# Banded attention with both key triangles in one square, in a two-layer decoder on one core

## The chip, the core and the metric

The kernel runs on one NeuronCore of a Trainium2 chip. The core has five engines that run side by side, each through its own queue in order: TensorE (PE, matmuls into PSUM, with its weight loads listed as PEld), VectorE (DVE), ScalarE (ACT), GpSimd (POOL) and SyncE (SP, which issues DMAs here). An instruction starts when it is at the head of its engine's queue and the semaphores it waits for have come. The metric is the device time of one launch in microseconds (us).

## What is computed

A trunk of two layers over 512 tokens of 1024 features, in float32. Layer 0 mixes positions with a gated MLP, layer 1 with windowed attention; both have a gated feed-forward part and a per-layer embedding. The change is in the attention of layer 1:

```python
def mixer_b(xn, w_q, sinks, w_o, kblk, vblk):
    q = (xn @ w_q).reshape(B, nb, BLOCK, N_KV_HEADS, GQA_GROUP, HEAD_DIM)
    scores = jnp.einsum('bnikgd,bnjkd->bnkgij', q, kblk) * (HEAD_DIM ** -0.5)
    dist = i + BLOCK - j
    in_band = (dist >= 0) & (dist < WINDOW)
    valid = in_band[None] & ((blk > 0) | (j[None] >= BLOCK))
    scores = scores - slopes * dist
    scores = jnp.where(valid, scores, -jnp.inf)
    m = jnp.maximum(jnp.max(scores, axis=-1, keepdims=True), sink)
    e = jnp.exp(scores - m)
    probs = e / (jnp.sum(e, axis=-1, keepdims=True) + jnp.exp(sink - m))
    out = jnp.einsum('bnkgij,bnjkd->bnikgd', probs, vblk)
    return out.reshape(B, S, N_Q_HEADS * HEAD_DIM) @ w_o
```

There are 16 query heads of 64 features in 4 groups, which share 4 key/value heads; 4 blocks of 128 queries; and a window of 128 keys. A query i of a block sees the keys j <= i of its own block and the keys j > i of the block before: two triangles that together fill one 128 x 128 square. The first block has no block before it. Each head has a sink, a logit without a value.

## The kernel before

Activations lie with features on the 128 partitions and tokens along the free axis. Every matrix product is made of three matmuls: a float32 number is split into a high half (rounded to the format in which PE multiplies at full pace) and a low half, and the products high x high, high x low and low x high are summed in PSUM. So each weight piece that a DMA brings (`wraw`) is cast by ScalarE (`wh`, line 157) and subtracted by VectorE (`wl`, line 158). `plan` lists the pieces in order of use, `load` issues their DMAs on SP's queue into three buffers of 8 KB per partition, and `pump` does the two splits up to four units of 1024 columns ahead of PE.

PSUM has eight banks of 512 columns, and all tiles rotate through them (`psum`). The order on each queue follows the program, moved a little by a scheduler: it puts instructions that are ready by its own estimate ahead, and `tc.high_priority()` lets a block go first.

The attention is a loop of 16 steps (line 786), one for a group g and a block n, with stages that overlap: at step i the scores of step i, the transposes of step i-1 and the value product of step i-2. Between them stands other PE work from a table, `beside`: the query projections of the later groups (`project`), the values of the later blocks (`values`) and the first parts of the output projection (`merge`).

- `scores` (line 701): per head, two matmuls of up to 256 columns against the keys of the previous and the own block (`kh`, `kl`), a fused VectorE operation that adds the position table `far` (with a huge distance outside the band), scales, and gives the minimum; then the exponential on ScalarE with its sum. `nsink` is the sink with its sign turned.
- `weights` (line 730): the sink's share, the reciprocal, and the multiplication, two heads on ScalarE and two on VectorE.
- `turn` (line 743): four transposes by PE for each of the two key blocks, then the split into halves (`ph`, `pl`, `pts`).
- `mix` (line 760): six matmuls of 256 columns for each key block, against value tiles `vth` and `vtl`, in which zeros stand beside the values so that two heads land on different partitions; then the split into `o2`.

The queries of group 0 are written by ScalarE and VectorE into place; those of later groups go through DMAs from SBUF to SBUF (`queries`). After the loop the output projection is finished, added to the residual `h`, and the next norm begins (`nf`, with sums of squares `nf1acc` on GpSimd). Further places with names used below: the value projections of layer 0 (`v`, into eight PSUM tiles, with the norm's `n0ms` between), and, at the end, the transposes of the residual (`ht`) between the gate's matmuls.

Of the kernel before, what the change touches and what calls it, by code (L numbers as in the profile page):

```python
# [9 lines left out]
F32R = mybir.dt.float32r  # L10
AF = mybir.ActivationFunctionType
# [32 lines left out]
UNIT = 1024  # L44
WBUFS = 4
# [5 lines left out]
def tile_yoco(ctx: ExitStack, tc: tile.TileContext, t, out: bass.AP, out_b: bass.AP):  # L51
# [15 lines left out]
    pieces = []  # L67

    def plan(ap_, n, cols, own=None):

        if own and len(own) > 1:
            m = n // len(own)
            cuts = [(q * m, m) for q in range(len(own))]
        else:
            m = n if n <= UNIT else (n // cols + 1) // 2 * cols
            cuts = [(0, m), (m, n - m)] if m < n else [(0, n)]
        pieces.append((ap_, n, cuts, own))
# [10 lines left out]
    def plan_ffn(l):  # L88
        for i, (j0, j1) in enumerate(PARTS):
            if i == 0:  # L90
                plan_cols(t["w_up"][l], j1, KD)
            else:
                plan_cols(t["w_up"][l, j0 + 1 : j1], j1 - j0 - 1, KD)
            if i + 1 < len(PARTS):
                plan_cols(t["w_up"][l, j1 : j1 + 1], 1, KD)
            else:
                plan(t["pT"][l], 2 * S, S, own=[(mp, "m4", "m5")])
                plan_cols(t["w_pin"][l], 2, 4)
            plan_cols(t["w_down"][l], 4, j1 - j0, k0=j0)
# [14 lines left out]
    plan_cols(t["w_o"], 4, KD)  # L114
# [7 lines left out]
    units = [(i, q, lo, n) for i, p in enumerate(pieces) for q, (lo, n) in enumerate(p[2])]  # L122
    raws, ready = {}, {}
    state = {"raw": 0, "unit": 0, "next": 0, "tags": [0, 1, 2], "turn": 0, "pt": 0}

    def load(upto, queue=nc.sync):
        while state["raw"] < min(upto, len(pieces)):
            j = state["raw"]
            a, m = pieces[j][:2]
            tags = state["tags"]  # L130
            r = wp.tile([P, 2 * UNIT], F32, tag=f"r{tags[state['turn'] % len(tags)]}", bufs=1, name=f"wraw{j}")
# [9 lines left out]
    def pump(upto):  # L141
        while state["unit"] < min(upto, len(units)):
            i, q, lo, n = units[state["unit"]]
            load(i + 1)
            u = state["unit"]
            own = pieces[i][3]
            if own:
                pool, *tags = own[q]
# [4 lines left out]
            src = raws[i][:, lo : lo + n]  # L153
# [57 lines left out]
    for i, (k0, k1) in enumerate(FIRST[1:]):  # L211
        load(i + 2)
        for k in range(k0, k1):
            nc.sync.dma_start(h[k], t["xT"][k])
    nc.sync.dma_start(vec[:, KD:], t["vec"][:, KD:])
# [266 lines left out]
    far = const.tile([P, 2 * P], F32, name="far")  # L482
    nc.gpsimd.iota(far, pattern=[[1, 2 * P]], base=-P, channel_multiplier=-1,
                   allow_small_or_imprecise_dtypes=True)
    nc.gpsimd.affine_select(out=far, in_=far, pattern=[[-1, 2 * P]], compare_op=ALU.is_ge,
                            fill=-FAR, base=P, channel_multiplier=1)
    nc.gpsimd.affine_select(out=far, in_=far, pattern=[[1, 2 * P]], compare_op=ALU.is_ge,
                            fill=-FAR, base=-1, channel_multiplier=-1)

    qscale = const.tile([P, KD], F32, name="qscale")  # L490
    for hd in range(HEADS):
        nc.gpsimd.memset(qscale[hd % 2 * HD : (hd % 2 + 1) * HD, hd // 2 : hd // 2 + 1], 1.0 / (8.0 * slope(hd)))
# [8 lines left out]
    nc.gpsimd.tensor_scalar_mul(nsink, sink, -1.0)  # L501

# [68 lines left out]

# [12 lines left out]
    rt = nm.tokens()  # L584

# [5 lines left out]
    mm3(qps[1], parts, xq, P)  # L591

    for j in range(2):
# [9 lines left out]
    def queries(ps, g, j):  # L603


        qf = tp.tile([P, S], F32, tag="sq", name=f"qf{g}_{j}")
        m = 2 * g + j
        nc.vector.scalar_tensor_tensor(qf, ps, qscale[:, m : m + 1], rstd, op0=ALU.mult, op1=ALU.mult)
        res = [tp.tile([P, S], F32R, tag=("hs", "sg", "c0", "c1")[2 * j + e], name=f"q{g}_{j}_{e}")
               for e in range(2)]  # L610
        if g == 0:
            for e, q in enumerate(res):
                me, it = sides[e], sides[1 - e]
                nc.scalar.copy(q[me, :], qf[me, :])
                nc.vector.tensor_sub(q[it, :], qf[me, :], q[me, :].bitcast(F32))
            return res

        hi = tp.tile([P, S], F32, tag="acc", name=f"qhi{g}_{j}")
        nc.scalar.copy(hi.bitcast(F32R), qf)
        nc.vector.tensor_sub(qf.bitcast(F32R), qf, hi)  # L620
        for e, q in enumerate(res):
            me, it = sides[e], sides[1 - e]
            nc.sync.dma_start(q[me, :].bitcast(F32), hi[me, :])
            nc.sync.dma_start(q[it, :].bitcast(F32), qf[me, :])
        return res

    qs = {0: []}
    for j in range(2):
        qs[0] += queries(qps[j], 0, j)

    VW = (NC * GROUPS * 2 + 1) * HD
    vt = [wp.tile([P, VW], F32R, tag="r2", bufs=1, name="vth"), at.tile([P, VW], F32R, tag="vtl", name="vtl")]
    for x, eng in zip(vt, (nc.gpsimd, nc.vector)):
        eng.memset(x[:, : VW - HD].rearrange("p (b w) -> p b w", w=2 * HD)[:, :, :HD].bitcast(F32), 0.0)
        eng.memset(x[:, VW - HD :].bitcast(F32), 0.0)

# [3 lines left out]
    def values(c):  # L642
        if c == 0:
            box["v"] = chunk(256, KD)
        ps = psum(f"vv{c}")
        mm3t(ps[:, :256], xkv, box["v"], 0, 256, c)
        pg = ps[:, :256].rearrange("p (g d) -> p g d", g=GROUPS)
        vh, vl = (x[:, : VW - HD].rearrange("p (c g w) -> p c g w", c=NC, g=GROUPS)[:, c, :, HD:] for x in vt)
        nc.scalar.activation(vh, pg, AF.Copy, scale=rt[:, c : c + 1])
        nc.vector.scalar_tensor_tensor(vl, pg, rt[:, c : c + 1], vh.bitcast(F32),  # L650
                                       op0=ALU.mult, op1=ALU.subtract)

    def project(g, j, k0, k1):
        if j == 0 and k0 == 0:
            box["q"] = chunk(256, KD)
            qs[g] = []
        if k0 == 0:
            box["qp"] = psum(f"q{g}_{j}")
        mm3(box["qp"], box["q"][k0:k1], xq[k0:k1], j * P, first=k0 == 0, last=k1 == KD)
        if k1 == KD:  # L660
            qs[g] += queries(box["qp"], g, j)

    def merge(m, k0, k1):

        if m // 2 not in box:
            box[m // 2] = chunk(256, KD)
        if k0 == 0:
            box[f"o{m}"] = psum(f"o{m}")
        mm3(box[f"o{m}"], box[m // 2][k0:k1], o2[k0:k1], m % 2 * P, first=k0 == 0, last=k1 == KD)
        box[f"k{m}"] = k1  # L670

    beside = {
        -1: [(values, 0), (values, 1)],
# [332 lines left out]
```

## Time and profile before

| | |
|---|---|
| median of 3 runs | 1159.05 us (1155.9 to 1159.5) |
| profiled execution, whole | 1159.21 us |
| its span in the profile | 1157.5 us |
| mean granted clock of TensorE | 0.993 |
| instructions | 13692 |
| weight traffic | HBM read 108.24 MB, 95 GB/s over the span |

A profile row for a group of instructions reads: line, engine, operation, what is written <- what is read, shapes, count | busy us, mean ns of one | idle time of the engine just before them and what ended it. A row of a timeline begins with the start and the length in us. A matmul's length reaches from its start until its results are in PSUM, and matmuls overlap, so their pace is read from starts, or from the chain of waits, where only the time that a link adds is counted.

### The profile page before, as it was taken

How to read it: one execution, taken by the hardware profiler on the slowest of the kernel's cores; microseconds unless marked ns; L12 is line 12 of the kernel's file. 1: busy time of each engine (PE TensorE's matmuls, PEld its weight loads, DVE VectorE, ACT ScalarE, POOL GpSimd, SP SyncE). 2: the span in 40 equal slices, each digit the busy share in tenths (PEclk: the TensorE clock that was granted, in tenths of full speed). 3: DMA queues.
4: the chain of work that ended last, by engine and by line, in shares of the span. 5: the costliest groups of instructions: out<-in, count | busy, mean ns of one | idle time of the engine just before them, and what ended most of it. 6: DMA issues, size and time to landing. Idle time of an engine off the chain costs nothing.

```text
span 1157.5 us, 13692 instructions
## 1 busy us (share of the span) xinstructions
PE 1139.6 (98%) x5408; PEld 956.2 (83%) x5408; DVE 744.3 (64%) x1138; ACT 524.3 (45%) x850; POOL 85.1 (7%) x92
## 2 busy tenths in 40 slices
PE   9999999999999999999999999999999999999996
PEld 7888888888888888888889888888888888888895
DVE  7356477763676377457868876677626763675666
ACT  6534344432443244555567874444413432445542
POOL 2100210000000000022300002100000000000232
PEclk9999999999999999999999999999999999999998
DMA  9322322322322333232133314232232233234302
GB/s 320 123 75 73 109 93 89 110 102 81 109 89 80 110 103 115 88 108 91 41 87 110 97 32 173 83 109 97 86 109 95 78 101 109 91 99 138 110 1 73
DMA packets 30735, 115.41 MB, mean 100 GB/s; under 512 B 3016, under 2 KB 14928, under 8 KB 21200
## 3 DMA queue, kind: packets, MB, share of 16 engines
q1 hardware_dynamic: 29552, 113.37, 29.3%
q10 hardware_dynamic: 1120, 1.18, 0.3%
q8 instruction: 42, 0.69, 0.3%
q14 instruction: 21, 0.17, 0.0%
HBM read 108.24 MB, written 2.11 MB: 95 GB/s over the span
## 4 chain that ended last, share of the span: by engine, by line
PE 93%; DVE 2%; DMA 1%; POOL 1%; issue 1%; ACT 1%; SPq 0%; POOLq 0%; ACTq 0%
PE up L186 14%; PE up L185 14%; PE up L184 14%; PE d L186 8%; PE d L185 8%; PE d L184 8%; PE gate L184 2%; PE gate L186 2%; PE gate L185 2%; PE pv L773 1%; PE o L184 1%; PE o L185 1%; PE o L186 1%; PE u L185 1%; PE u L184 1%; PE u L186 1%
## 5 line engine op out<-in xcount | busy, mean ns | idle before, releaser
L158 DVE TENSOR_TENSOR wl<-wraw,wh 128x1024 fp32r<-128x1024 f32 (+2 forms) x197 | 237.8, 1209 | 130.7 <-ACT wh L157 120.7
L157 ACT CAST wh<-wraw 128x1024 fp32r<-128x1024 f32 (+1 forms) x196 | 201.5, 1032 | 235.6 <-PE d L185 131.6
L184 PE MATMUL up<-nf00h,wh 128*128 128x512 f32 x352 | 137.1, 390 | 0.0
L184 PE MATMUL up<-nf10h,wh 128*128 128x512 f32 x352 | 137.0, 389 | 0.0
L185 PE MATMUL up<-nf00l,wh 128*128 128x512 f32 x352 | 136.9, 389 | 0.0
L185 PE MATMUL up<-nf10l,wh 128*128 128x512 f32 x352 | 136.9, 389 | 0.0
L186 PE MATMUL up<-nf00h,wl 128*128 128x512 f32 x352 | 136.9, 389 | 0.0
L184 PE MATMUL d<-ah,wh 128*128 128x512 f32 x352 | 136.9, 389 | 0.0
L185 PE MATMUL d<-al,wh 128*128 128x512 f32 x352 | 136.9, 389 | 0.0
L186 PE MATMUL d<-ah,wl 128*128 128x512 f32 x352 | 136.9, 389 | 0.0
L186 PE MATMUL up<-nf10h,wl 128*128 128x512 f32 x352 | 136.9, 389 | 0.0
L361 ACT ACTIVATE c<-hs,vec 128x512 f32<-128x512 f32 x88 | 71.6, 814 | 85.8 <-DVE hs L357 85.0
L362 DVE SCALAR_TENSOR_TENSOR c<-hs,vec,c 128x511 f32<-128x511 f32 x88 | 65.8, 748 | 35.8 <-ACT c L361 35.6
L335 DVE TENSOR_TENSOR h<-h,d 128x512 f32<-128x512 f32 x56 | 38.4, 686 | 74.1 <-PE d L186 74.1
L245 ACT CAST ah<-a 128x512 fp32r<-128x512 f32 x44 | 27.3, 621 | 114.8 <-DVE a L367 114.8
L184 PEld LDWEIGHTS up<-nf10h,wh 128*128 128x128 f32 x352 | 66.1, 188 | 13.8
L184 PEld LDWEIGHTS d<-ah,wh 128*128 128x128 f32 x352 | 66.1, 188 | 13.8
L185 PEld LDWEIGHTS up<-nf00l,wh 128*128 128x128 f32 x352 | 66.1, 188 | 13.7
L185 PEld LDWEIGHTS d<-al,wh 128*128 128x128 f32 x352 | 66.1, 188 | 13.7
L185 PEld LDWEIGHTS up<-nf10l,wh 128*128 128x128 f32 x352 | 66.1, 188 | 13.7
L186 PEld LDWEIGHTS up<-nf00h,wl 128*128 128x128 f32 x352 | 66.1, 188 | 13.7
L184 PEld LDWEIGHTS up<-nf00h,wh 128*128 128x128 f32 x352 | 66.1, 188 | 13.6
(309 smaller groups left out, 2078.7 us busy)
## 6 DMA issues: line engine op xcount, KB each, us to landing
wraw<-in_w_up SPq DMA_DIRECT2D x44, 1024.0 KB, 4.8
wraw<-in_w_down SPq DMA_DIRECT2D x16, 896.0 KB, 4.6
wraw<-in_w_down SPq DMA_DIRECT2D x8, 1024.0 KB, 5.1
wraw<-in_w_u SPq DMA_DIRECT2D x4, 1024.0 KB, 6.5
wraw<-in_w_out SPq DMA_DIRECT2D x4, 1024.0 KB, 4.9
wraw<-in_w_gate SPq DMA_DIRECT2D x4, 1024.0 KB, 4.8
wraw<-in_w_q SPq DMA_DIRECT2D x4, 1024.0 KB, 5.0
wraw<-in_w_o SPq DMA_DIRECT2D x4, 1024.0 KB, 6.2
```

Source lines behind the costliest of these rows:

```text
L157: nc.scalar.copy(wh[:, :n], src)
L158: nc.vector.tensor_sub(wl[:, :n], src, wh[:, :n].bitcast(F32))
L184: nc.tensor.matmul(ps, wh[:, a:b], xh, start=st, stop=False)
L185: nc.tensor.matmul(ps, wh[:, a:b], xl, start=False, stop=False)
L186: nc.tensor.matmul(ps, wl[:, a:b], xh, start=False, stop=en)
L245: nc.scalar.copy(hi, src)
L335: nc.vector.tensor_add(h[m], h[m], ps)
L361: nc.scalar.activation(c, hs, AF.Identity, bias=v("conv_b", l * 2 * NJ + col), scale=cw[2])
L362: nc.vector.scalar_tensor_tensor(c[:, 1:], hs[:, : S - 1], cw[1], c[:, 1:], op0=ALU.mult, op1=ALU.add)
L773: nc.tensor.matmul(ps, lhs, rhs[:, :, e, :], start=first, stop=end)
```

## The change

It rewrites the attention loop, its preparation, the PSUM pool and the loads.

- **One square.** The scores of four heads go to one PSUM tile of two banks (`psum2`). Where j > i, `copy_predicated` copies the previous block's scores over the own block's (mask `above`), so that one square of 128 keys holds both triangles. One `scalar_tensor_tensor` for four heads multiplies by `rq` (the query's norm and 1/8) and adds `alibi` (slope times distance, made by GpSimd once per group); one `tensor_reduce` takes the minimum. The sink is a 129th column, so its exponential and sum come with the others. In the first block of a group the triangle j > i is filled with a huge number (`away`).
- **Weights and transposes.** The multiplication by the reciprocal is one GpSimd operation for four heads. There are four transposes per step, not eight; ScalarE makes the high half, VectorE the low one, and GpSimd's `affine_select` makes copies of both with only the triangle j > i.
- **Values.** A value tile holds the high and low halves side by side in 128 columns (`vt`), so one weight load serves both; `vd` holds the previous block's values minus the own block's, in the same way. A step is `vt` x all weights + `vd` x the triangle: four matmuls of 512 columns (two in a first block). The rows from the low halves then lie on partitions 64 to 127: ScalarE copies them down (`low_rows`) and VectorE adds (`outputs`).
- **Order.** All values are computed ahead of the loop; the queries of all groups go through DMAs; `beside` now has single products of the projection (three matmuls) and half output projections (`w_o` is planned in two halves, and each half is added to `h` by itself). High priority is gone.
- **PSUM.** Two banks belong to the scores; the other six rotate as four `mm`, one `tr`, one `pv`.
- **Loads.** Each unit of up to 1024 columns has its own DMA and buffer: six buffers of 4 KB per partition for three of 8 KB.

```diff
-    mmp = ctx.enter_context(tc.tile_pool(name="mmp", bufs=8, space=bass.MemoryType.PSUM))
-    def psum(name):
-        return mmp.tile([P, S], F32, tag="mm", name=name)
+    banks = {"at": 0, "tags": ["mm", "mm", "mm", "mm", "tr", "pv"]}
+    def psum(name, tag=None):
+        if tag is None:
+            tag = banks["tags"][banks["at"] % len(banks["tags"])]
+            banks["at"] += 1
+        return mmp.tile([P, S], F32, tag=tag, bufs=4 if tag == "mm" else 1, name=name)
+    def psum2(name):
+        return mmp.tile([P, 2, S], F32, tag="sc", name=name)
...
-    plan_cols(t["w_o"], 4, KD)
+    for k0 in (0, 4):
+        plan_cols(t["w_o"], 4, 4, k0=k0)
...
-            r = wp.tile([P, 2 * UNIT], F32, tag=f"r{tags[state['turn'] % len(tags)]}", bufs=1, name=f"wraw{j}")
+            r = wp.tile([P, UNIT], F32, tag=f"r{tags[state['turn'] % len(tags)]}", bufs=1, name=f"wraw{j}")
...
+    def halves(dst, src):
+        x = src.rearrange("p (g d) -> p g d", g=GROUPS)
+        nc.scalar.copy(dst[:, :, :HD], x)
+        nc.vector.tensor_sub(dst[:, :, HD:], x, dst[:, :, :HD].bitcast(F32))
+    for c in range(NC):
+        ps = psum(f"vv{c}")
+        mm3t(ps[:, :256], xkv, parts, 0, 256, c)
+        nc.scalar.activation(vf[c], ps[:, :256], AF.Copy, scale=rt[:, c : c + 1])
+        halves(vt[c // 2][:, c % 2], vf[c])
+        if c:
+            nc.gpsimd.tensor_sub(d, vf[c - 1], vf[c])
+            halves(vd[:, c - 1], d)
...
     def scores(i):
+        sc = psum2(f"sc{i}")
...
+    def logits(i, o):
+        cur = o[:, :, P:]
+        nc.gpsimd.tensor_copy(pr[:, :, P], nsink[:, GQ * g : GQ * (g + 1)])
+        if n:
+            nc.vector.copy_predicated(cur, above.bitcast(U32).unsqueeze(1).to_broadcast([P, GQ, P]), o[:, :, :P])
+        nc.vector.scalar_tensor_tensor(pr[:, :, :P], cur, rq[:, n : n + 1], alibi, op0=ALU.mult, op1=ALU.add)
+        if n == 0:
+            nc.vector.copy_predicated(pr[:, :, :P], above.bitcast(U32).unsqueeze(1).to_broadcast([P, GQ, P]),
+                                      away.unsqueeze(1).to_broadcast([P, GQ, P]))
+        nc.vector.tensor_reduce(low, pr, axis=mybir.AxisListType.X, op=ALU.min)
...
     def weights(i):
+        nc.vector.reciprocal(sm, sm)
+        nc.gpsimd.tensor_mul(pr[:, :, :P], pr[:, :, :P], sm.unsqueeze(2).to_broadcast([P, GQ, P]))
...
+    def turned_lo(i, tr):
+        nc.vector.tensor_sub(pl, tr, ph.bitcast(F32))
+        if n:
+            for a, b in ((ph, mh), (pl, ml)):
+                nc.gpsimd.affine_select(out=b, in_=a.bitcast(F32), pattern=[[0, GQ], [-1, P]], compare_op=ALU.is_gt,
+                                        fill=0.0, base=0, channel_multiplier=1)
...
     def mix(i):
+            terms = [(cur, ph), (dif, mh), (cur, pl), (dif, ml)]
+        for a, (lhs, rhs) in enumerate(terms):
+            nc.tensor.matmul(ps, lhs, rhs, start=a == 0, stop=a == len(terms) - 1)
...
+    for i, n in enumerate((6, 5, 5, 5, 5, 5, 5, 4, 4, 4)):
+        beside[i] = [(project, u + a) for a in range(n)]
+    for a, ms in enumerate(((0,), (1, 2), (3,), (4,), (5, 6), (7,))):
+        beside[10 + a] = [(merge, m, 0, 4, True, True) for m in ms]
```

How instructions move on the queues, at three places. First PE in the loop, before: the end of a step's transposes (`tr`) and its value product (`pv`), with the scores (`sc`) of a later step put between; a suffix of digits is a tile's number.

```order
L716 MATMUL sc_2_4916<-kl_4201,q_1_0_4604 128x256
L750 MATMUL tr_1_4894<-ident,pr_4710 128x128 x2
L773 MATMUL pv_4870<-pts_4476,vth 128x256
L773 MATMUL pv_4870<-pts_4476,vtl 128x256
L773 MATMUL pv_4870<-pts_4476,vth 128x256 x2
L773 MATMUL pv_4870<-pts_4476,vtl 128x256
L773 MATMUL pv_4870<-ph_1_4813,vth 128x256
L773 MATMUL pv_4870<-pl_1_4814,vth 128x256
L773 MATMUL pv_4870<-ph_1_4813,vtl 128x256
L715 MATMUL sc_0_4909<-kh_4199,q_0_1_4539 128x256
```

The same engine in the changed kernel, in step 8: the last scores, the value product, fill (`q`, the projection of the next group), and the transposes.

```order
L691 MATMUL sc_5185<-kh_4286,q_1_1_5058 128x128
L691 MATMUL sc_5185<-kl_4288,q_1_1_5058 128x128
L767 MATMUL pv_5194<-ph_5153,vt_4487 128x512
L767 MATMUL pv_5194<-pm_5155,vd 128x512
L767 MATMUL pv_5194<-pl_5154,vt_4487 128x512
L767 MATMUL pv_5194<-pm_5155,vd 128x512
L190 MATMUL q_1_5207<-n11h_3914,wh_4687 128x512
L191 MATMUL q_1_5207<-n11l_3915,wh_4687 128x512
L192 MATMUL q_1_5207<-n11h_3914,wl_4688 128x512
```

The value product has four wide matmuls in place of twelve, stands right behind the scores of a step, and reads what GpSimd has made (`pm`).

Second, VectorE in the loop of the changed kernel, from one step's predicated copy to the next one's (`pb` are the two output adds, `low` the minimum, `wl` a weight split, `pl` the low half of the transposed weights, `sm` the reciprocal).

```order
L701 COPY_PREDICATED sc_4970<-above,sc_4970 128x4x128
L702 SCALAR_TENSOR_TENSOR prs<-sc_4970,rq,alibi 128x4x128
L785 TENSOR_TENSOR pb_4990<-pv_4979,pb_4990 64x2x128
L707 TENSOR_REDUCE low_4987<-prs 128x4
L785 TENSOR_TENSOR pb_4990<-pv_4979,pb_4990 64x2x128
L164 TENSOR_TENSOR wl_4890<-wraw_4887,wh_4889 128x1024
L750 TENSOR_TENSOR pl_5011<-tr_4998,ph_5010 128x512
L721 RECIPROCAL sm_4989<-sm_4989 128x4
L701 COPY_PREDICATED sc_5028<-above,sc_5028 128x4x128
```

Between the minimum and the reciprocal lie the exponentials on ScalarE; the next step's copy stands behind the reciprocal.

Third, PE near the end: the transposes of the residual. Before, all sixteen stand ahead of the fifth gate tile; in the changed kernel the last of them stand so:

```order
L899 MATMUL ht_0_8826<-ident,h_80 128x128
L899 MATMUL ht_0_8826<-ident,h_81 128x128
L899 MATMUL ht_0_8826<-ident,h_82 128x128
L899 MATMUL ht_0_8826<-ident,h_83 128x128
L190 MATMUL gate_8929<-np10h_5951,own_ah_8841 128x256
L191 MATMUL gate_8929<-np10l_5952,own_ah_8841 128x256
L192 MATMUL gate_8929<-np10h_5951,own_al_8842 128x256
L190 MATMUL gate_8929<-np10h_5953,own_ah_8848 128x256
L899 MATMUL ht_1_8832<-ident,h_84 128x128
```

Eight transposes come ahead of the first bank that VectorE frees by reading a gate tile, and the third and fourth tile of transposes wait for banks, the fourth behind four matmuls of the gate.

More of the change, by code (lines that the diff above doesn't have):

```diff
@@ L627, in tile_yoco @@
[L627 to L637, printed above, removed]
-    box = {}
[L642 to L651, printed above, removed]
@@ L743, in turn @@
[L743 to L758 removed]
+            for a, (x, st) in enumerate(((kh, True), (kl, False))):
+                nc.tensor.matmul(o[:, e, 2 * P - nk :], q, x[g // 2][:, g % 2, t0 : t0 + nk], start=st, stop=not st)
@@ L786, in tile_yoco, with fill @@
+    def fill(i, a, b):
+        for f, *args in beside[i][a:b]:
+            f(*args)
+    slopes(0)
+    pump(state["next"] + WBUFS)
     for i in range(last + 2):
         if i < last:
-            with tc.high_priority():
-                scores(i)
-        fill(i)
+            o = scores(i)
         if i >= 2:
-            mix(i - 2)
+            pv = mix(i - 2)
+        if i < last:
+            logits(i, o)
+        if i >= 2:
+            pb = low_rows(i - 2, pv)
+        early = 2 if i < 10 else 1
+        fill(i, 0, early)
@@ new lines, in tile_yoco @@
+        if 0 <= i - 1 < last:
+            turned_hi(i - 1, tr)
+        if i < last:
+            exps(i, (1, 2, 3))
+        if 0 <= i - 1 < last:
+            turned_lo(i - 1, tr)
+        fill(i, early, None)
+        pump(state["next"] + WBUFS - 1)
+        if i < last:
+            if i % 4 == 3 and i + 1 < last:
+                slopes(i // 4 + 1)
+            weights(i)
+    state["tags"] = list(range(RAWS))
+    nf = Norm("nf1", [(xp, "x", gain("norm_ffn", 1))])
+    for m in range(KD):
+        if m < 5:
+            merge(m, 6, 8, False, True)
+        else:
+            merge(m, 4, 8, True, True)
+        nf.take(m)
```

319 lines of the change are left out of this document (147 added, 172 removed).

## The prediction

> **What bounds the kernel now.** I read the page's engine totals first, then who waits on TensorE (PE), then the attention stage in time windows.
>
> ```profile
> span 1157.5 us, 13692 instructions
> PE 1139.6 (98%) x5408; PEld 956.2 (83%) x5408; DVE 744.3 (64%) x1138; ACT 524.3 (45%) x850; POOL 85.1 (7%) x92
> PE sc L715 <- DVE q L615: 2.0, 1, 2.0
> PE sc L715 <- DMA q<-qf: 2.0, 2, 1.5
> PE sc L715 <- DVE neg L718: 0.5, 1, 0.5
> ```
>
> PE is busy all but 18 us; the rest is start and end. The waits (us in total, times, longest) that the change can reach all stand at the scores: 4.5 us. So time is won by fewer matmuls, as long as no new wait replaces them.
>
> ```profile
> 570.50:728.50 158.00, 153.37 (x893) 134.12 (x892) 117.12 (x331) 106.49 (x288) 13.63 (x11) 0.98 0.32 94
> 670.00:672.00 2.00, 2.00 (x10) 1.68 (x10) 1.07 (x6) 1.14 (x6) 0.00 (x0) 0.82 0.00 0
> 672.00:674.00 2.00, 2.00 (x6) 1.51 (x6) 0.83 (x4) 0.87 (x4) 0.00 (x0) 0.50 0.00 0
> 674.00:676.00 2.00, 2.00 (x15) 1.80 (x14) 0.43 (x1) 1.51 (x2) 0.00 (x0) 0.83 0.00 0
> ```
>
> These windows give length, busy time of PE, PEld, DVE, ACT, POOL, then PE's granted clock. The first is the whole stage, from the first query matmul to the last output projection: 158.0 us, 4.63 us without PE work, clock 0.98 on average. The others follow the 1.5 us wait for the query DMA: the clock falls to a half for some 3.4 us, which costs 2 x (0.18 + 0.50 + 0.17) = 1.7 us on top. An idle gap is dear.
>
> **What PE gives up.** Busy times of overlapping matmuls can't be added, so I take the pace from the chain of waits (start, us, count):
>
> ```profile
> 18.33 0.91 PE v L195 x4
> 676.32 1.31 PE pv L773 x11
> 690.74 0.87 PE tr L750 x8
> ```
>
> That is 0.2275 us for 512 columns, 0.119 for 256, 0.109 for a transpose. The counts:
>
> ```profile
> L773 PE MATMUL pv<-pts,vth 128*128 128x256 f32 x76 | 17.0, 291 | 0.0
> L773 PE MATMUL pv<-pts,vtl 128*128 128x256 f32 x38 | 10.7, 283 | 0.0
> L773 PE MATMUL pv<-pl,vth 128*128 128x256 f32 x18 | 5.4, 300 | 0.0
> L773 PE MATMUL pv<-ph,vtl 128*128 128x256 f32 x18 | 5.1, 285 | 0.0
> L773 PE MATMUL pv<-ph,vth 128*128 128x256 f32 x18 | 5.1, 281 | 0.0
> L750 PE MATMUL tr<-ident,pr 128*128 128x128 f32 x112 | 18.3, 273 | 0.0
> ```
>
> 168 value matmuls x 0.119 = 20.0 us become 12 steps x 4 + 4 x 2 = 56 of 512 columns, 12.7 us; 112 transposes, 12.2 us, become 64, 7.0 us. Unchanged: queries and output projection, 384 x 0.2275 = 87.4; values, 96 x 0.119 = 11.4; scores, 128 x 0.119 = 15.2. So the stage holds 146.2 us of PE work before and 133.7 after, 12.5 less. Its other 11.8 us are the 4.63 of waits, 0.02 x 158 = 3.2 of slow clock, and 4.0 of gaps, mostly where transposes and scores alternate.
>
> **The new round of each step.** Head by head work becomes one chain per step: copy_predicated, scalar_tensor_tensor, one of the two output adds and the minimum on DVE, four exponentials on ACT (with two output casts and often the cast of the transposed weights between them), the reciprocal back on DVE; behind it in DVE's queue stands the next step's copy_predicated. The rows nearest to these:
>
> ```profile
> L246 DVE TENSOR_TENSOR pts<-tr,pts 128x512 fp32r<-128x512 f32 x19 | 13.0, 686 | 2.1 <-ACT pts L245 2.0
> L608 DVE SCALAR_TENSOR_TENSOR qf<-q,qscale,n1rstd 128x512 f32<-128x512 f32 x8 | 6.0, 749 | 3.4 <-PE q L186 3.4
> L819 DVE TENSOR_TENSOR z<-gate,np1rstd 128x256 f32<-128x256 f32 x8 | 3.3, 418 | 0.4 <-PE gate L186 0.3
> L309 DVE TRANSPOSE_TENSOR_REDUCE nf1fold<-nf1acc 128x16 f32<-128x512 f32 x1 | 0.7, 711 | 0.0
> L734 DVE RECIPROCAL ds<-ds 128x4 f32<-128x4 f32 x16 | 2.8, 173 | 0.3
> L158 DVE TENSOR_TENSOR wl<-wraw,wh 128x1024 fp32r<-128x1024 f32 x179 | 221.1, 1237 | 121.9 <-ACT wh L157 111.9 <-PE v L197 9.7
> L723 ACT ACTIVATE pr<-pr,neg 128x128 f32<-128x128 f32 x16 | 6.4, 398 | 3.2 <-DVE neg L718 2.9
> L723 ACT ACTIVATION_READ_ACCUMULATOR pr<-pr,neg 128x1 f32 x64 | 12.1, 188 | 0.0
> L779 ACT CAST oh<-pv 128x128 fp32r<-128x128 f32 x32 | 8.2, 255 | 3.0 <-DVE ol L780 1.9 <-PE pv L773 0.9
> L245 ACT CAST pts<-tr 128x512 fp32r<-128x512 f32 x19 | 11.1, 582 | 5.6 <-PE tr L750 3.4 <-PE pv L773 2.0
> ```
>
> No row shows copy_predicated. Below, it is an ordinary pass of 512 with an input in PSUM, 0.69; above, two such passes, 1.37, since it keeps part of its output; nothing suggests under 0.69. I take 0.69, the row of its own size and operands' kind. DVE: 0.69 + 0.75 + 0.42 + 0.71, less three overlaps of about 0.06, is 2.39. ACT: 4 x (0.398 + 0.188) + 2 x 0.255 + 0.582 = 3.44. With the reciprocal, 0.17, the round is T = 6.0 us; where the cast of the transposed weights comes ahead of the exponentials, 5.4. PE's own step: scores 0.95, values 0.91, transposes 0.44, and 15 projection matmuls (3.41) early, 12 (2.73) later: 5.71 or 5.03; 0.46 less when the step mixes a first block. Over the 18 steps, steps 0 and 1 pipeline, 11 and 14 hold 24 matmuls and are PE's; the other twelve wait 2 x 0.75 + 3 x 0.29 + 3 x 0.97 + 1.42 + 3 x 0.97 = 9.6 us. Most of the 12.5 us is thus given back, because in these steps PE has too little to do beside the round. What waits there is the next scores: their pair of PSUM banks is single, and they need scalar_tensor_tensor to have read it; behind them in PE's queue stand the value matmuls and all the fill of that step.
>
> GpSimd gets the multiplication by the reciprocal, the two triangle selections, four slope tables per group and two low halves per step:
>
> ```profile
> L275 POOL TENSOR_TENSOR nf1acc<-nf1acc,nf1sq 128x512 f32<-128x512 f32 x5 | 7.2, 1446 | 10.9 <-ACT nf1sq L270 10.8
> L503 POOL TENSOR_SCALAR_AFFINE_SELECT wsT<-wsT 128x1024 f32<-128x1024 f32 x1 | 1.6, 1644 | 20.5 <-DMA wsT<-in_wsT 20.5
> L831 POOL TENSOR_TENSOR facc<-facc,fsq 128x256 f32<-128x256 f32 x6 | 4.6, 760 | 5.8 <-ACT fsq L826 5.7
> ```
>
> 1.45 + 2 x 0.82 + 2 x 0.42 is 3.9 us a step: inside T. From the transposes of a step to its last value matmul lie 0.58 + 2 x 0.82 + 0.84 = 3.1 us with some hops, against some 3.8 us in which PE does fill and the next scores; that cover is thin. What GpSimd does to DVE, beside which it was idle in this loop, one place shows:
>
> ```profile
> 706.45 1.77 POOL L275 TENSOR_TENSOR nf1acc<-nf1sq,nf1sq 128x512 f32<-128x512 f32 x1 [130.71 <-DVE h L804]
> 707.07 0.69 DVE L804 TENSOR_TENSOR h<-h,o 128x512 f32<-128x512 f32 x1
> 708.96 3.20 POOL L275 TENSOR_TENSOR nf1acc<-nf1acc,nf1sq 128x512 f32<-128x512 f32 x2 [0.74 <-ACT nf1sq L270]
> 709.22 3.49 DVE L242 SCALAR_TENSOR_TENSOR nf10l<-h,vec,nf10h 128x512 fp32r<-128x512 f32 x2
> ```
>
> The add with one operand in PSUM kept its 0.69 under GpSimd's 1.77; two operations with both operands in SBUF took 3.49 instead of 2 x 0.75. The Trainium skill ("SBUF — State Buffer", section "SBUF: two separate sides") says that the pair of ports that VectorE and GpSimd share is an exclusive lock, taken also by a VectorE operation with two SBUF inputs against a GpSimd one that reads SBUF; the trace agrees. In the new round only the ten weight splits (wl) in the loop are of that kind. Waiting a whole 1.45 us, each is 2.69 us long; with the second add and the low half of the weights (0.36 + 0.63) that is 3.7 beside ACT's 3.4, so little in most steps: I take none, and 0.75 each, 7.5 us in all, as the upper bound.
>
> **The rest.** The last step drains with less fill. Behind its scores PE holds 6.6 us of other work, but its transposes can come only after 7.4 (2.39 on DVE, 2.9 on ACT, 0.17, GpSimd's 1.45, and hops): 0.8 late. Then 1.4 us of projection stand against the cast, the low half and the second selection, 0.58 + 0.69 + 0.82: another 0.8 with a hop. Together 1.6. The values now precede the loop, so queries and keys have their DMAs behind 11.4 us of PE work, and each later group is projected over a step ahead: the 4.5 us of waits and their slow clock go. But the value halves stand ahead of the first logits on DVE: 0.5. I leave one slow-clock window, 1.7, for the new gaps, and 1.0 of the old 4.0, as scores and transposes no longer alternate. The Trainium skill ("TensorE: Matmul & The Clock Gate", section "What's actually happening") puts the fall after at least one idle window of about 3.4 us; here 1.5 us of idling sufficed, and by the page's rule the 1.7 would be nothing.
>
> Six PSUM banks rotate instead of eight. Two places feel it:
>
> ```profile
> 34.63 0.48 PE L195 MATMUL v<-wh,n00h 128*128 128x512 f32 x1
> 34.82 0.17 DVE L316 TENSOR_SCALAR n0m<-n0ms 128x16 f32<-128x16 f32 x1 [3.48 <-PE n0ms L289]
> 1110.43 1.91 PE L856 MATMUL ht<-ident,h 128*128 128x128 f32 x16
> 1112.81 0.39 PE L184 MATMUL gate<-np10h,own_ah 128*128 128x256 f32 x1 [0.47 <-DVE z L819]
> ```
>
> The second value tile at 34.63 must now wait for DVE's read, done at 34.99: 0.4. Of the sixteen transposes at 1110.43, eight go behind the gate's first read, so half of 1.91 us moves past the wait: 0.95, and the end with it. Half-size loads I cost at nothing:
>
> ```profile
> wraw<-in_w_pin SPq DMA_DIRECT2D x4, 512.0 KB, 3.4
> ```
>
> 3.4 us for 512 KB, against 24 x 0.2275 = 5.5 us of matmuls per such piece, with six buffers; what hides a load is that lead of several pieces. Without it, as right after the loop, where two buffers are free until the last value matmul, a late piece would cost up to 3.4; the 15 us of output projection that follow cover it.
>
> **Sum.** Stage after: 133.7 + 9.6 + 1.6 + 0.5 + 1.7 + 1.0 = 148.1, so 9.9 less; plus 0.4 and 0.95: 8.55 us faster. The profiled execution took 1159.21 us, 1.7 around its span and 0.16 above the median of the runs, so no correction is needed: **1150.7**.
>
> **Rivals.** *Cover holds* (0.20): casts ahead of the exponentials, T below PE's step; the 9.6 and the 1.7 vanish: 1139.4. For it: 5.4 is possible; against: many steps have the cast between. *No change* (0.11): T near 6.6, by GpSimd's thin cover; 12 x 0.6 = 7.2 more: 1157.9. *Slower* (0.21): the round DVE to ACT to DVE is the bound by more than its cover. With copy_predicated at 1.37, T is 6.7: 12 x 0.68 = 8.2; with the ten locked splits 7.5 more: 1166.4. It decides from T = 6.0 + 8.55/12 = 6.7 on. For it: the 3.49 above; against: most of the round's operands are in PSUM. The forecast has 0.48.
>
> **Numbers.** A difference under 0.3%, 3.5 us, can't be told from none. Faster: 0.48 + 0.20 = 0.68; same 0.11; slower 0.21. The range runs from the case of full cover, 1140, to near the slower case, 1163; the forecast's own is 1144 to 1156.
>
> **What would show it.** Right: 56 value matmuls near 0.23 us apart and 64 transposes; PE's waits at scores and values each under 1 us, on DVE or POOL; no wait on a query DMA; a stage of 145 to 151 us. Wrong: copy_predicated well over 0.7 us, ScalarE waiting long for the minimum, value matmuls waiting for the selections, or a granted clock at a half in much of the loop.

## The result and the profile after

The changed kernel took 1154.12 us in the median of 7 runs (1151.23 to 1154.35), the kernel before beside it 1158.12 (7 runs, 1155.9 to 1160.56): a ratio of 0.996, with a 95% interval from 0.9945 to 0.9974. It is some 4 us faster where 8.55 were forecast. The profiled executions are 5.1 us apart in span. The page's totals:

```profile
span 1152.4 us, 13748 instructions
PE 1130.3 (98%) x5248; PEld 938.4 (81%) x5248; DVE 737.9 (64%) x984; ACT 508.8 (44%) x811; POOL 148.6 (13%) x181
```

PE has 160 matmuls and 9.3 us of busy time less, and 4 us more without work. Who it waited for (us in total, times, longest):

```profile
PE pv L767 <- POOL pm L753: 2.7, 5, 0.8
PE tr L729 <- POOL prs L722: 2.3, 3, 1.3
PE ht L899 <- DVE z L861: 1.8, 1, 1.8
...
PE up L191 <- DVE nf10l L249: 1.0, 2, 0.6
...
PE up L190 <- ACT nf10h L248: 0.6, 1, 0.6
...
PE nf1ms L296 <- DVE nf1fold L316: 0.2, 1, 0.2
```

The waits for queries and at the scores are gone. New ones stand at the value product and the transposes, both for GpSimd, and at two places behind the attention: the first tiles of the feed-forward part (`up`) and the transposes at the end (`ht`). The attention stage, and then the windows behind it (length, busy time of PE, PEld, DVE, ACT, POOL, granted clock, DMA share, GB/s):

```profile
571.50:716.00 144.50, 139.06 (x732) 114.24 (x731) 107.39 (x175) 87.86 (x246) 73.06 (x109) 1.00 0.39 117
...
720.00:722.00 2.00, 1.20 (x5) 0.34 (x3) 2.00 (x3) 0.52 (x1) 0.30 (x1) 1.00 0.82 260
722.00:724.00 2.00, 1.20 (x3) 0.69 (x3) 1.97 (x4) 0.72 (x2) 0.00 (x0) 0.80 0.19 57
724.00:726.00 2.00, 1.78 (x6) 1.20 (x5) 0.76 (x2) 0.00 (x0) 0.39 (x1) 0.50 0.54 207
726.00:728.00 2.00, 2.00 (x6) 1.52 (x6) 0.00 (x0) 0.00 (x0) 2.00 (x1) 0.50 0.00 0
728.00:730.00 2.00, 2.00 (x7) 1.52 (x6) 1.39 (x2) 0.00 (x0) 0.54 (x1) 0.50 0.00 0
```

The stage, from the first query matmul to the first matmul of `up`, went from 157.7 us (570.48 to 728.17) to 144.5: 13.2 us less, more than the 9.9 of the forecast. Then 5.8 are given back: the 36th matmul of `up` came 8.18 us after the first before (728.17 to 736.35) and comes 13.99 after it now (716.00 to 729.99): 1.8 us of waits (the rows of `up` and `nf1ms` above), with VectorE busy without a gap until 724.6, and six to seven matmuls in 2 us, where the clock is a half, instead of ten. With 1.05 us ahead of the stage and 1.24 at the end (from `np1ms` to the token half of the gate, 16.38 us before, 17.62 now): 1.05 - 13.2 + 5.8 + 1.24 = -5.1, the whole difference of the spans.

The groups that the prediction priced, and those that turned out to matter:

```profile
L715 ACT ACTIVATE prs<-prs,low 128x129 f32<-128x129 f32 x64 | 25.3, 398 | 8.5 <-DVE low L707 8.5
...
L722 POOL TENSOR_TENSOR prs<-prs,sm 128x512 f32<-128x512 f32 x16 | 18.8, 1174 | 1.3 <-DVE sm L721 0.8 <-PE pv L767 0.4
...
L753 POOL TENSOR_SCALAR_AFFINE_SELECT pm<-pp 128x512 fp32r<-128x512 f32 x16 | 12.8, 800 | 15.5 <-ACT pp L744 14.8 <-DVE pp L750 0.8
...
L715 ACT ACTIVATION_READ_ACCUMULATOR prs<-prs,low 128x1 f32 x64 | 12.1, 189 | 0.0
...
L249 DVE SCALAR_TENSOR_TENSOR nf10l<-h,vec,nf10h 128x512 fp32r<-128x512 f32 x8 | 9.9, 1242 | 0.1
...
L701 DVE COPY_PREDICATED sc<-above,sc 128x512 f32<-128x512 uint32 x12 | 8.2, 686 | 2.6 <-PE sc L691 2.5
...
L282 POOL TENSOR_TENSOR nf1acc<-nf1acc,nf1sq 128x512 f32<-128x512 f32 x5 | 7.6, 1527 | 4.4 <-ACT nf1sq L277 4.2
```

Two readings decide the loop. No row of PE's waits stands at the scores, and the last column of the `copy_predicated` row says that VectorE idles 2.6 us in all before it, in five of the twelve steps, until PE's scores come. In those steps VectorE waits for PE, and in none does PE wait for VectorE there. One round in the timeline of VectorE (start, length), and the first of ScalarE's four exponentials in it:

```profile
605.83 0.70 DVE L701 COPY_PREDICATED sc<-above,sc 128x512 f32<-128x512 uint32 x1 [0.31 <-PE sc L691]
606.63 0.75 DVE L702 SCALAR_TENSOR_TENSOR prs<-sc,rq,alibi 128x512 f32<-128x512 f32 x1
...
607.63 0.67 DVE L707 TENSOR_REDUCE low<-prs 128x4 f32<-128x516 f32 x1
...
610.52 0.17 DVE L721 RECIPROCAL sm<-sm 128x4 f32<-128x4 f32 x1
611.12 0.70 DVE L701 COPY_PREDICATED sc<-above,sc 128x512 f32<-128x512 uint32 x1 [0.43 <-PE sc L691]
```
```profile
608.58 0.41 ACT L715 ACTIVATE prs<-prs,low 128x129 f32<-128x129 f32 x1
608.88 0.19 ACT L715 ACTIVATION_READ_ACCUMULATOR prs<-prs,low 128x1 f32 x1
608.98 0.40 ACT L715 ACTIVATE prs<-prs,low 128x129 f32<-128x129 f32 x1
```

From the copy to the end of the reciprocal are 4.86 us, and 0.43 of idling follow. This is the shortest round: the ones that begin at 600.22, 611.12, 624.43, 629.60 and 635.25 took 5.30, 5.59, 5.25, 5.74 and 5.69 us, and later ones, with more of VectorE's other work in them, up to 7.5. An exponential with its sum takes 0.40 from start to start, not 0.398 + 0.189: reading the accumulator overlaps with the operations on both sides. The profile before shows the same:

```profile
620.70 0.40 ACT L723 ACTIVATE pr<-pr,neg 128x128 f32<-128x128 f32 x1
621.01 0.18 ACT L723 ACTIVATION_READ_ACCUMULATOR pr<-pr,neg 128x1 f32 x1
621.10 0.39 ACT L723 ACTIVATE pr<-pr,neg 128x128 f32<-128x128 f32 x1
```

### The profile page after: what moved, and what is told of

Its sections match the earlier page's. It is cut to its first block, busy times and chain, and to the rows that moved or that the text cites. A ratio compares the mean times of both kernels' runs of the same rounds, so it can differ in the third digit from the quotient of the medians.

```text
span 1152.4 us, 13748 instructions
## 1 busy us (share of the span) xinstructions
PE 1130.3 (98%) x5248; PEld 938.4 (81%) x5248; DVE 737.9 (64%) x984; ACT 508.8 (44%) x811; POOL 148.6 (13%) x181
## 4 chain that ended last, share of the span: by engine, by line
PE 88%; DVE 4%; ACT 3%; POOL 2%; issue 1%; DMA 1%; SPq 0%; POOLq 0%; ACTq 0%; DVEq 0%
PE up L190 14%; PE up L191 14%; PE up L192 14%; PE d L190 8%; PE d L192 8%; PE d L191 8%; PE gate L190 2%; PE gate L192 2%; PE gate L191 2%; PE u L192 1%; PE u L190 1%; PE u L191 1%; PE v L202 1%; PE v L203 1%; PE v L201 1%
## 5 line engine op out<-in xcount | busy, mean ns | idle before, releaser
L192 PEld LDWEIGHTS up<-nf10h,wl 128*128 128x128 f32 x352 | 66.8, 190 | 14.0
L192 PEld LDWEIGHTS d<-ah,wl 128*128 128x128 f32 x352 | 66.1, 188 | 13.8
```

Source lines behind the costliest of these rows:

```text
L192: nc.tensor.matmul(ps, wl[:, a:b], xh, start=False, stop=en)
```

## The experiments

Each is the changed kernel with one edit, unless it says otherwise. Four of them leave the stage as it is (the second, fourth, seventh and ninth): it took them 145.7, 144.8, 144.9 and 144.7 us, so with the changed kernel's own 144.5 a stage that nothing touched varies by 1.2 us. Total times vary more; the clock is one reason, as the changed kernel's fastest execution (1151.23 us) has a mean granted clock of 0.997 and those around 1154 have 0.994 to 0.995. The kernel before, run beside each group of runs, took 1157.3 to 1158.8, so runs of different groups are compared by their ratios to it; the changed kernel's is 0.996.

**1. The predicated copy twice.**

```diff
             nc.vector.copy_predicated(cur, ..., o[:, :, :P])
+            nc.vector.copy_predicated(cur, ..., o[:, :, :P])
```

> The changed kernel, with the predicated copy of the twelve steps that have a block before them done twice; the second finds what the first wrote, so nothing else changes. Theory of the prediction (the round DVE, ACT, DVE binds in twelve steps): the round is 0.69 us longer in each, so the attention stage (first query matmul to first matmul of the feed-forward part) goes from 144.5 to some 152.5 us, 12 x 0.69 = 8.3. Rival (PE's own work and its fill set the pace in most steps, and the round has slack): the stage grows by under 2.5 us. In between, by so many steps as the round binds.

1160.43 us (11 runs), ratio to the kernel before 1.0014 (1.0005 to 1.0023); the stage took 149.4 us. The waits:

```profile
PE pv L768 <- POOL pm L754: 6.1, 8, 2.3
PE tr L730 <- POOL prs L723: 3.0, 7, 1.0
```

4.9 us are between the two: as much as seven of the twelve additions came through, and none at the scores, where the prediction had them. They came through GpSimd, whose multiplication and selections stand behind the round. PE's own step is mostly 5.0 to 5.9 us long (between the starts of scores, in steps without a wait or a double share of fill), so rounds of 4.9 to 5.7 us that grow by 0.69 pass it in some steps and not in others. That this is why seven came through is an argument; no run shows it step by step.

**2. Without GpSimd's adds of squares.**

```diff
-            if self.acc is None:
+            if self.acc is None or self.name == "nf1" and k < KD - 1:
```

> The changed kernel without the six GpSimd adds (nf1acc) that sum the squares for the norm behind the attention: that norm is made from the last two of its eight squares, the rest is left out. Theory (lock): the adds stretch nf10l from 0.75 to 1.78 us and wl from 1.22 to 1.72, 4.9 us on a VectorE that is busy without a gap from 704 to 724; without them the last low halves come 4.9 us earlier, PE's waits at up (1.8 us) and the half clock behind them go, and the kernel is some 5.5 us faster than the changed one: 1148.5. Rival (cover too short): 15 us of output projection behind the loop are too little for VectorE's 20 us of work even at full pace: the waits stay in part, 1151 to 1153. Second rival (late loads of w_up, whose buffers come free only with the last value product): no change, 1154.

1148.49 us (4 runs), ratio 0.9913 (0.99 to 0.9927). `nf10l` and the window that had been idle and at a falling clock:

```profile
L249 DVE SCALAR_TENSOR_TENSOR nf10l<-h,vec,nf10h 128x512 fp32r<-128x512 f32 x8 | 5.9, 747 | 0.4 <-ACT nf10h L248 0.4
```
```profile
722.00:724.00 2.00, 2.00 (x11) 1.66 (x11) 0.17 (x1) 0.00 (x0) 1.12 (x1) 1.00 0.00 0
```

The theory's number came, and PE has no wait at `up`. Late loads are out: they were not touched. (PE waits once at the scores in this run, 0.7 us for VectorE. In the changed kernel and the other ten runs it never does; in three of them it waits there 0.2 to 0.3 us for a query's DMA.) What the run doesn't tell is whether the stretched operations must go or whether it is enough that PE does not stand behind them; that took runs 7 and 9.

**3. Half of the embedding product as cover.**

```diff
     for m in range(KD):
         ...
         nf.take(m)
+    ple_in_both(0)
```

(The weights of that half are planned in the new order; its six PSUM tiles are the scores' two banks, `tr` and `pv`.)

> The changed kernel, with the first half of the embedding product of layer 1 (24 matmuls of 256 columns and 12 of 512, 5.6 us of PE, which need nothing of the attention) taken from the end of the feed-forward part to the place between the output projection and the feed-forward part. Theory (the norm's halves come late for want of cover): 5.6 us of cover hold the 4 us by which the last halves are late; the waits at up and the half clock go, 5.5 us faster than the changed kernel: 1148.5. Rival: the stall moves to the place that the product left, where now 5.6 us of it in place of 11.2 cover the last activation: same as the changed kernel, 1154.

1152.46 us (5 runs), ratio 0.9945 (0.9933 to 0.9958). The waits at `up` went, but a new one came:

```profile
PE pinf L195 <- ACT pef L430: 2.8, 1, 2.8
```

Between the matmuls PE waits for ScalarE's copy of an earlier one, which stands in ScalarE's queue behind the late norm. The cover works; the cover's own output waits for the engine that it was to cover. The theory's 1148.5 was missed by 4 us, the rival named another place, and the ratio can't be told from the changed kernel's.

**4. The end's transposes in the scores' banks.**

```diff
+        pair = psum2("ht") if i == 0 else None
+        hps = [psum(f"ht{i}_{q}") if i else pair[:, q] for q in range(2)]
...
-            ps = psum(f"ht{i}_{q}")
```

> The changed kernel, with the first eight of the sixteen transposes at the end (ht) in the two PSUM banks of the scores, which are free by then, so that twelve of them, not four, stand ahead of VectorE's first read of the gate. Theory (six rotating banks are what the end lost): eight transposes more in the wait are 0.87 us, the wait of 1.78 us falls to 0.9 and with it the half clock behind it: 0.9 to 1.3 us faster than the changed kernel, 1153. Rival (the wait is for VectorE's z in any case): no change.

1152.78 us (5 runs), ratio 0.9947 (0.9935 to 0.996). PE's wait at `ht` is 0.9 instead of 1.8 us, and the stretch from `np1ms` to the token half of the gate 16.8 instead of 17.6, against 16.4 before. The theory, a little under its range, as far as the wait goes. The half clock that it put behind the wait was not there to be removed; in the changed kernel:

```profile
1106.47 1.09 PE L899 MATMUL ht<-ident,h 128*128 128x128 f32 x8 [1.78 <-DVE z L861]
```
```profile
1106.00:1108.00 2.00, 1.53 (x14) 1.53 (x15) 1.75 (x5) 1.55 (x4) 0.12 (x1) 1.00 0.00 0
```

The interval of the total alone would not tell this run from the changed kernel.

**5. The multiplication on VectorE.**

```diff
-        nc.gpsimd.tensor_mul(pr[:, :, :P], ...)
+        nc.vector.tensor_mul(pr[:, :, :P], ...)
```

> The changed kernel, with the multiplication of the weights by the reciprocal on VectorE in place of GpSimd (1.17 us on the mean there). Theory (GpSimd's queue makes PE wait: 2.7 us for the selections pm and 2.3 us for the weights prs): both shrink, and the stage from the first query matmul to the feed-forward part falls from 144.5 us to 141.5 to 143. Rival (the round DVE, ACT, DVE binds): 0.75 us more on VectorE in each step act like the second predicated copy, which made the stage 4.9 us longer: 148 to 150.

1153.02 us (6 runs), ratio 0.9957 (0.9942 to 0.9973), stage 143.7. The rival is out in so far as 16 x 0.705 us more on VectorE lengthened nothing. But the edit also shortens the chain behind the round, by GpSimd's 1.17 us a step, so it does not test a longer round as run 1 does. And the waits only moved (`pm` 2.4, `prs` on VectorE 0.6, the cast `pp` on ScalarE 0.8), and 0.8 us is within what stages differ by.

**6. The slope tables on ScalarE.**

```diff
-            nc.gpsimd.tensor_scalar_mul(alibi[:, e, :], dist, slope(GQ * g + e))
+            nc.scalar.activation(alibi[:, e, :], dist, AF.Copy, scale=slope(GQ * g + e))
```

> The changed kernel, with the four slope tables of a group (alibi, 2.3 us of GpSimd at each change of group) made by ScalarE. Three of PE's five waits for pm (0.70, 0.70 and 0.78 us) come in the step after such a change. Theory (the selections are late because the tables stand ahead of them on GpSimd): these waits go, 2.2 us: the stage falls from 144.5 to some 142.3. Rival (ScalarE's place in the round counts more): four operations of about 0.25 us, three times, are 3 us more on ScalarE: the stage is the same or up to 3 us longer.

In the changed kernel, GpSimd at the first change of group:

```profile
613.15 2.31 POOL L679 TENSOR_SCALAR alibi<-dist 128x128 f32<-128x128 f32 x4 [0.16 <-DVE prs L702]
615.53 1.37 POOL L753 TENSOR_SCALAR_AFFINE_SELECT pm<-ph 128x512 fp32r<-128x512 f32 x1
```

`ph` was ready at 614.55, and PE waited 0.70 us for the selections at 618. In this run the waits for `pm` are 1.3 us, 1.4 less: the two of 0.70 us are gone, and the 0.78 stays. The expectation read that one wrongly: in the changed kernel it ends at 658.99, ahead of the third table, which begins at 661.48. It has another cause, a selection that takes 1.44 us beside a weight split of VectorE:

```profile
657.22 1.23 DVE L164 TENSOR_TENSOR wl<-wraw,wh 128x1024 fp32r<-128x1024 f32 x1
657.50 1.44 POOL L753 TENSOR_SCALAR_AFFINE_SELECT pm<-pp 128x512 fp32r<-128x512 f32 x1 [2.71 <-ACT pp L744]
658.99 0.50 PE L767 MATMUL pv<-pm,vd 128*128 128x512 f32 x1 [0.78 <-POOL pm L753]
```

So the theory holds for the two waits that do follow a table. The stage is 143.3, 1.2 less, which by itself is no more than untouched stages vary. 1152.32 us (5 runs), ratio 0.9948 (0.9934 to 0.9963). The profiled execution, 1150.6, is the fastest of the five, for a reason that lies elsewhere. Behind the attention it idles as the changed kernel does, and the clock stays:

```profile
717.00:720.00 3.00, 2.55 (x12) 1.80 (x11) 3.00 (x3) 1.71 (x3) 1.43 (x2) 1.00 0.28 100
720.00:722.00 2.00, 1.12 (x3) 0.38 (x3) 2.00 (x3) 1.25 (x2) 0.00 (x0) 1.00 0.28 113
722.00:724.00 2.00, 1.01 (x5) 0.60 (x5) 1.54 (x3) 0.00 (x0) 0.00 (x0) 1.00 0.66 223
724.00:726.00 2.00, 2.00 (x10) 1.66 (x10) 0.17 (x1) 0.00 (x0) 1.62 (x1) 1.00 0.10 39
```

**7. The adds of squares on VectorE.**

```diff
-            self.square(k)
+            self.square(k, nc.vector if self.name == "nf1" else None)
```

> The changed kernel, with the six adds of squares behind the attention (nf1acc) on VectorE. Nothing is left out. Theory (lock): VectorE gets 6 x 0.68 = 4.1 us of adds and loses 4.9 us of stretched operations, so PE's stall at up is about the same: the kernel equals the changed one within 1 us, 1153 to 1154. Rival (the adds cost by their own latency on GpSimd, not by what they do to VectorE): most of the 5 us that leaving them out gave are won here too: 1149 to 1150.

1148.02 us (5 runs), ratio 0.9915 (0.99 to 0.993): the expectation from the lock missed by over 5 us. VectorE's last low half ends at 721.4, 5.7 us after the first `up`; in the changed kernel 7.2. That is 1.5 us earlier, and still 0.7 after the 23rd matmul of `up`, 22 x 0.2275 behind the first, should have had it. The rest is an order that changed by itself. PE's queue at the end of the first `up` tile (a suffix of digits numbers a tile; 5824 and 5826 are the norm's last two):

```
L192 MATMUL up_0_5981<-nf10h_5824,wl_5809 128x512
L190 MATMUL up_1_6012<-nf10h_5812,wh_5802 128x512
L190 MATMUL up_0_5981<-nf10h_5826,wh_5808 128x512
L191 MATMUL up_1_6012<-nf10l_5813,wh_5802 128x512
L192 MATMUL up_1_6012<-nf10h_5812,wl_5803 128x512
L190 MATMUL up_1_6012<-nf10h_5814,wh_5802 128x512
L191 MATMUL up_1_6012<-nf10l_5815,wh_5802 128x512
L191 MATMUL up_0_5981<-nf10l_5827,wh_5808 128x512
```

In the changed kernel all of `up_0` comes first. The scheduler orders by its own estimate. A likely reading, which no run shows, is that with the adds among VectorE's instructions it takes the norm to be late, and with the adds on GpSimd it does not see that VectorE will be. So neither theory of this run was right, and order and lock had to be parted.

**8. The cover of run 3, its copies behind all its matmuls, and the banks of run 4.**

> The changed kernel, with the half of the embedding product ahead of the feed-forward part, its copies on ScalarE behind all its matmuls (PE waited 2.8 us for such a copy between them in the run before), and with the transposes at the end in the scores' PSUM banks. Theory (two stalls, each for want of cover): 5.5 and 0.9 us less than the changed kernel: 1147.5 to 1148, which beats both kernels. Rival (the wait for the copies only goes to the first up tiles): as the run with the half product alone less 0.9: 1151.

1149.01 us (5 runs), ratio 0.9922 (0.9909 to 0.9936), between the two.

```profile
PE up L195 <- ACT pet L446: 1.6, 1, 1.6
```

The wait for the copies went to the `up` tile that needs a bank, as the rival said, but a good part smaller.

**9. PE's order alone.**

```diff
+            pss = [psum(f"up{j}_{s}") for s in range(2)]
+            if j == 0 and l:
+                for s in range(2):
+                    mm3(pss[s], parts[:6], xs[:6], s * P, last=False)
+            for s, ps in enumerate(pss):
+                if j == 0 and l:
+                    mm3(ps, parts[6:], xs[6:], s * P, first=False)
...
```

> The changed kernel, with only PE's order in the first pair of tiles of the feed-forward part (up) changed: the products of the first six norm tiles for both, 36 matmuls or 8.2 us, then those of the last two. GpSimd's adds stay, and VectorE's operations stay stretched. Theory (PE waits because the last two norm tiles stand at the head of its queue, while work of the second up tile is ready): the waits at up (1.8 us) and the half clock behind them go, as when the adds were moved and the order moved by itself: some 5 us faster than the changed kernel, 1148 to 1149. Rival (the lock itself has to go; the norm's factor comes later and stalls the tiles behind): less than 2 us faster.

1148.01 us (5 runs), ratio 0.9917 (0.9903 to 0.993). VectorE is as slow as ever, and PE does not care:

```profile
L249 DVE SCALAR_TENSOR_TENSOR nf10l<-h,vec,nf10h 128x512 fp32r<-128x512 f32 x8 | 9.9, 1244 | 0.1
```
```profile
722.00:724.00 2.00, 2.00 (x10) 1.65 (x10) 1.97 (x4) 1.51 (x2) 0.00 (x0) 1.00 0.33 102
```

About what leaving the adds out gave. GpSimd's adds make the norm late, but that costs only because PE's queue had nothing else in front of it.

**10. Four edits together:** runs 4, 6 and 9, and the multiplication on VectorE in the last step only.

```diff
-        nc.gpsimd.tensor_mul(pr[:, :, :P], ...)
+        (nc.gpsimd if i < last - 1 else nc.vector).tensor_mul(pr[:, :, :P], ...)
```

> The changed kernel with four edits: PE's order in the first up tiles, the eight transposes at the end in the scores' PSUM banks, the slope tables on ScalarE, and in the last step alone the multiplication on VectorE (there PE waits 1.33 us for GpSimd's 2.09 us). If the costs are separate they add: 5.0 + 0.9 + 1.2 + 1.2 = 8.3 us off 1154.1, so 1146, some 12 us or 1.0% under the kernel before. Rival (they share cover, and the fall of the clock comes anyway with one of the waits left): 1148 to 1150.

1144.28 us (4 runs), ratio 0.9886 (0.9873 to 0.99): 1.1% under the kernel before, and clear of the changed kernel's interval. The costs add: by the two ratios the four edits give some 8.6 us, where 8.3 were added up. The stage is 141.7 us, and PE's waits in it are

```profile
PE pv L772 <- POOL pm L758: 1.5, 3, 0.8
PE tr L734 <- POOL prs L727: 1.0, 2, 0.5
```

**11. Without the predicated copy.**

```diff
         if n:
-            nc.vector.copy_predicated(cur, ..., o[:, :, :P])
+            pass
```

> The changed kernel without the predicated copy: the previous block's scores are not taken into the square, so a query attends to the later keys of its own block; everything else runs as before. Theory after the runs so far (VectorE, ScalarE and VectorE need 4.9 us for a round, under PE's 5.0 to 5.9 us a step, so the round is covered): the stage, 144.5 us, loses only part of its 5.2 us of waits, 1 to 3 us. Rival (the prediction's: the round binds in twelve steps): 12 x 0.69 = 8.3 us less, 136.

1151.06 us in one run; stage 141.7, 2.8 less, with 2.4 us of waits for GpSimd instead of 5.0. The round does not bind at the scores: of 12 x 0.686 = 8.2 us taken out of it, a third comes through, and the waits for GpSimd shrink by about as much.

## Why the prediction was half right

The direction was right and the time 3.4 us too low. That it came so close is luck in good part: 9.6 us of waits at the scores did not come, and 5.0 us of waits for GpSimd, longer gaps and 5.8 us behind the stage came in their place. Of the prediction's own signs of being wrong one is there: value matmuls wait for the selections, 2.7 us in all.

- **PE's work, right.** 56 value products and 64 transposes are there, and each new price on VectorE was met: 0.686 for `copy_predicated` (0.69), 0.747 for the scaling, 0.673 for the minimum.
- **The round, wrong.** The step "ACT: 4 x (0.398 + 0.188)" adds two durations that overlap; from start to start it is 0.40. With the 0.75 us less that this makes, the prediction's own sum gives a round of 5.25 us, not 6.0, and 2.0 us of waits, not 9.6; the trace has rounds of 4.9 to 5.7 in the early steps, and of "the other twelve wait" nothing came at the scores. The round counts as the head of a chain that ends in GpSimd: 0.69 us more in each of twelve rounds cost 4.9 (run 1), as much less gave 2.8 (run 11). The rival with the full cover, at 0.20, had the scores right, but its stage of 136.8 us was missed by 7.7, more than the forecast's 148.1 by 3.6.
- **GpSimd, warned of and not priced.** The prediction called that cover thin and took 3.9 us a step as hidden. The slope tables of three groups, the multiplication and two selections in one queue make PE wait 5.0 us at the value product and the transposes. 1.33 and 0.25 of it are the last steps' drain, for which 1.6 was forecast. Run 6 shows the tables' part, 1.4; run 10 brings these waits to 2.5. Three of the waits (0.26, 0.78 and the 1.33) follow an operation of GpSimd's that took long beside a weight split of VectorE's: selections of 1.56 and 1.44 us where 0.64 is usual, a multiplication of 2.09 where 1.04 is. The prediction asked what the two do to VectorE in the loop and took none; it was GpSimd that lost the time.
- **Gaps and clock.** The stage's 144.5 us are 133.7 of work, 5.4 without PE work, and 5.4 of gaps too short for the view of waits: reckoned from starts, a value product follows another after 0.28 us on the mean instead of 0.2275. The forecast allowed 1.0 for such gaps and 1.7 for a slow clock; the clock stayed at 1.00 in the stage and fell behind it.
- **Behind the stage, missing.** The words "the 15 us of output projection that follow cover it" were said of late loads, and no load is waited for. But the same work is also all the cover of the norm, and from the last value product to the first `up` there are now 18.7 us (697.3 to 716.0), not 27.5 (700.7 to 728.2): from 704.6 to 724.6 VectorE works without a gap on residual adds, `nf10l` and weight splits, four of eight `nf10l` stretched to 1.74 us on the mean, the longest 1.79, beside GpSimd's adds. The prediction quoted the 3.49 us that show this lock, at this very place, and used it for the loop alone. Runs 2 and 9 show the cause, GpSimd's adds and PE's order, and the price: 5.8 us in the profiled execution, 5.0 to 5.4 by the ratios of runs 2, 7 and 9. It is the largest cost that the forecast did not have.
- **PSUM banks.** At the start a value tile waits 0.3 us for `n0m` (0.4 forecast), but the first query comes 1.05 later. That is partly chance: in the runs above it comes at 570.6 to 571.7, against 570.48 before. At the end only four transposes, not eight, stand ahead of VectorE's first read of the gate. The other twelve go behind it, and PE waits 1.78 us instead of 0.47: 1.24 longer for the 0.95 that was forecast, all of it the wait, as the granted clock stayed at 1.00.

So -9.9 + 0.4 + 0.95 became -13.2 + 1.05 + 1.24 + 5.8.

## What to carry to other kernels

Take the length of a chain from start to start in a timeline, not from a sum of mean durations, which overlap. When work is taken out of a stage, go through everything that this work covered, the next stage's norm too, and not only the transfers. When an operand may be late, put work that is ready in front of it in PE's queue: that took no work away and gave about as much here as the change itself (some 5 us).

## What had not been expected of the hardware

- **The clock after short waits.** 1.8 us of PE waits within 4 us were followed by 7 us at half clock in the profiled run. 2.3 us at the same place in run 6 were not, nor were single waits of 1.33 us in the last step, 1.78 at `ht` and 2.8 in run 3. The Trainium skill ("TensorE: Matmul & The Clock Gate", section "What's actually happening") calls the gate's window free-running, which agrees with such chance; its fall after at least one idle window of about 3.4 us does not, as no wait at that place is that long.
- **Both sides are slowed.** `nf10l` took 0.74 us alone and up to 1.79 beside GpSimd's adds. A selection on GpSimd took 0.64 at 617.70 in the changed kernel, and 1.37 at 615.53 and 1.44 at 657.50, while VectorE did a weight split.
- **A conditional copy at an ordinary price.** 0.686 us for 128 x 512 between PSUM operands, and 0.685 at the second time in run 1, though it keeps part of what it writes.
